# A linear-attention and MLP layer on one core: two token halves of a head scaled together and later, the first gate pass's block adds on VectorE, turned low parts issued later

## Chip, core and metric

The kernel runs on one core of a Trainium2 chip. TensorE multiplies matrices into PSUM, VectorE, ScalarE and GpSimd (POOL in the profile) work on SBUF and PSUM, and DMA queues move data; SP issues most DMAs. The metric is the device time in microseconds of one execution. Each engine runs its own instructions strictly in the order in which the program issued them; between engines they wait for each other's semaphores.

## What is computed

The reference, cut to what runs (DEPTH is 1, so the only layer is the gated linear attention, followed by the MLP and a last RMSNorm):

```python
def _gla_mixer(h, w_in, w_gate_up, b_gate, o_norm, w_out):
    proj = h @ w_in
    q, k, v, r, g_low = jnp.split(proj, [...], axis=-1)
    log_a = jax.nn.log_sigmoid((g_low @ w_gate_up + b_gate)) / GLA_GATE_TEMP
    ...
    def step(state, xs):                       # over chunks of 64 tokens
        q_c, k_c, v_c, d_c = xs
        state = d_c[..., None] * state + jnp.einsum('bhck,bhcv->bhkv', k_c, v_c)
        return state, jnp.einsum('bhck,bhkv->bhcv', q_c, state)
    ...
    o = o * lax.rsqrt(jnp.mean(o * o, axis=-1, keepdims=True) + EPS) * o_norm
    return (o * jax.nn.silu(r)) @ w_out

def reference(x, ...):
    h = x + _gla_mixer(_rmsnorm(x, gla_norm), ...)
    h = h + jnp.square(jax.nn.relu(_rmsnorm(h, mlp_norm) @ w_up)) @ w_down
    return _rmsnorm(h, final_norm)
```

256 tokens, model width 2048, 4 heads with 256 key and 512 value columns each, MLP width 8192, all in float32.

## The kernel before

**Products in three parts.** Every float32 weight is loaded raw and split in two: ScalarE casts it to a rounded *high* part, VectorE subtracts that from the raw weight for the *low* part. TensorE then multiplies high by high, low by high and high by low. A group of 512 weight rows x 512 columns (1 MB, the tile of 128 x 2048) is called a *double* in the code. A *plain* double is 48 matmuls of 256 columns. A *summed* double does the same with 42 after the scheme of Strassen and Winograd: it needs sums of the four 256-column blocks of the weights, and of the inputs.

**The stage of the change** begins where the projections q, k, v and the scores are done. It runs four passes over w_in for the gate r (c = 0 to 3, 512 columns each, 4 doubles per pass), then four over w_out. In this text the doubles are numbered in their order: 0 to 3 are pass 0 (0 and 2 plain, 1 and 3 summed), 4 to 7 pass 1 (plain), 8 to 11 pass 2 (8 and 10 plain, 9 and 11 summed), 12 to 15 pass 3 (plain), 16 and on w_out. The raw weights of double n go into `rawu0`, `rawu1` or `rawu2` (n mod 3; 2346, 2347 and 2348 in the order of instructions), its parts into `high` and `low` of three slots, also n mod 3. A load waits for the low part three doubles back, which is the last to read the raw tile.

**Summed doubles.** For each, POOL issues a DMA that adds one block to another within the raw tile (`add_block`, L843), then VectorE forms three sums (`adds`), ScalarE casts them into `sumshl`, and VectorE subtracts (`low`, L520). The high part of the whole raw tile also waits for the added block.

**Heads.** Between the steps of pass 0, TensorE computes the attention output of the four heads, each in two halves of 128 tokens (`attend`, 6 matmuls for half 0, 12 for half 1), every one into a PSUM bank of its own. For each half, `attend_square` lets ScalarE square it and sum the squares into `oss`; VectorE scales that one column; POOL raises it to -0.5 (`rsqrt`, L314, the *power*) and multiplies by `r1k` (L888, the *product*). `attend_put` then lets ScalarE write the scaled half into `on` (the *put*, L893) and gives the bank back. There are eight banks (named aux_1893, aux_1894, acc_1763 to acc_1766, acc_1895, acc_1896); they are handed out in the order in which they come back. Pass 0 holds four of them: t0, t1, b16 and b50.

**Combining.** At the end of a summed pass, `combine_parts` copies b16 (L932), adds and subtracts the banks on VectorE, and ScalarE applies silu (L965).

**Turned parts.** `on` and later h are transposed on TensorE; of each transposed block, ScalarE writes the high part and VectorE the low part (`put_turned`).

**What sets the order.** `at(time, run)` puts a piece of work into `plan`; the plan is sorted by time and issued in that order, and this is the order on every engine. The unit of time is one matmul. TensorE's steps stand in it from -LENGTH on; weights have fixed offsets to their use (high -75, low -56 for a plain double; high -67, low -50, sums -68 for a summed one).

Of the kernel before, what the change touches and what calls it, by code (L numbers as in the profile page):

```python
# [27 lines left out]
F32 = mybir.dt.float32  # L28
F32R = mybir.dt.float32r
AF = mybir.ActivationFunctionType  # L30
ALU = mybir.AluOpType

P = 128
T = 256
NT = T // P
# [4 lines left out]
DV = 512  # L40
# [30 lines left out]
def tile_gla_mlp(ctx, tc, x, xt, w_vg, w_in, w_gate, w_out, w_up, w_down, final_norm, out):  # L71
    nc = tc.nc
# [3 lines left out]
    st = ctx.enter_context(tc.tile_pool(name="st", bufs=4))  # L76
# [219 lines left out]
    r1k = const.tile([P, NT], F32, name="r1k")  # L296
# [16 lines left out]
    def rsqrt(dst, ms):  # L313
        nc.gpsimd.tensor_tensor(dst, ms, mhalf, op=ALU.pow)  # L314
# [303 lines left out]
    def at(time, run):  # L618
        plan.append((time, len(plan), run))
# [125 lines left out]
    def turned_part(key, n):  # L745
        return turn_banks[key][n // 2][:, n % 2 * T : (n % 2 + 1) * T]

    def put_turned(key, n, to, gain):
        s = turned_part(key, n)
        nc.scalar.activation(to[0], s, AF.Copy, scale=gain)  # L750
        nc.vector.scalar_tensor_tensor(to[1], s, gain, to[0].bitcast(F32), op0=ALU.mult, op1=ALU.subtract)
        if n % 2:
            banks.append(turn_banks[key][n // 2])
# [77 lines left out]
    for n, (p, c, g, summed_) in enumerate(doubles):  # L831
# [14 lines left out]
            chunk(key, time - UP_HI, time - UP_LO, time + 2 * UP, (time - UP_EARLY, load), raw)  # L846
            continue
        chunk(key, time - 67, time - 50, time + RAWS, (time - 165, load), raw)
        at(time - 116, add_block)

        def adds(view=view):
            add(sums[:, 0], view[:, :, 1, left], view[:, :, 0, left])
            add(sums[:, 1], sums[:, 0], view[:, :, 0, right])
            sub(sums[:, 2], sums[:, 0], view[:, :, 1, right])
# [23 lines left out]
        attend_state[hd, t] = o  # L878

    def attend_square(hd, t):  # L880
        o = attend_state[hd, t]
        ss = st.tile([P, 1], F32, tag="oss", name="oss")
        sq = tmp.tile([P, DV], F32, tag="t512", name="sq", bufs=3)
        nc.scalar.activation(sq, o, AF.Square, scale=r1k[:, t : t + 1], accum_out=ss)
        nc.vector.tensor_scalar(ss, ss, 1.0 / DV, EPS, op0=ALU.mult, op1=ALU.add)
        rs = st.tile([P, 1], F32, tag="ors", name="ors")
        rsqrt(rs, ss)
        nc.gpsimd.tensor_tensor(rs, rs, r1k[:, t : t + 1], op=ALU.mult)  # L888
        attend_state[hd, t] = o, rs

    def attend_put(hd, t):
        o, rs = attend_state[hd, t]
        nc.scalar.activation(on[:, t, hd * DV : (hd + 1) * DV], o, AF.Copy, scale=rs)  # L893
        banks.append(o)

    for hd, t, time in attend_at:
        at(time - LENGTH + 1, lambda hd=hd, t=t: attend_square(hd, t))
        at(time - LENGTH + 27, lambda hd=hd, t=t: attend_put(hd, t))


    def some512():
# [88 lines left out]
    def row_o(kt):  # L990
        return [a[:, OFF + kt * T : OFF + (kt + 1) * T] for a in (oth, otl)]
# [19 lines left out]

    e = mark("turn o0") + 16
    for n in range(8):
        at(e + 1 + 9 * n, lambda n=n: put_turned("o0", n, row_o(n), gain_o(n)))

    e = mark("turn o1") + 16
    for m, g in enumerate((2, 3)):
# [74 lines left out]
    def row_h(kt):  # L1092
        return [a[:, kt * T : (kt + 1) * T] for a in turned_h]
# [1 line left out]
    e = mark("turn h0") + 16  # L1095
    at(e - 17, take_h)
    for n in range(8):
        at(e + 1 + 9 * n, lambda n=n: put_turned("h0", n, row_h(n), g2(n)))

    def turn_h1():  # L1100
        bs = turn_banks["h1"] = [bank_in_parts() for _ in range(4)]
        for n, kt in enumerate(range(8, 16)):
            for t in range(NT):
                nc.tensor.transpose(bs[n // 2][:, n % 2 * T + t * P : n % 2 * T + (t + 1) * P], h[:, t, kt * P : (kt + 1) * P], ident)
        for n in (0, 2, 1, 3, 4, 6, 5, 7):
            put_turned("h1", n, row_h(8 + n), g2(8 + n))

    at(0.5, room_for_mlp)
    at(47.5, turn_h1)
# [478 lines left out]
```

## Time and profile before

| | |
|---|---|
| three runs | 1056.58, 1056.63, 1057.29 us; median 1056.63 |
| the profiled execution | 1056.8 us |
| its span, first to last instruction | 1055.0 us |
| mean granted TensorE clock | 0.997 |
| DMA, mean over the span | 217 GB/s |
| doubles 0 to 3 with the heads | TensorE from 190.81 us |

The profile names an instruction by line, engine, operation and tiles, output first; tile names are without their numbers there (`rawu` is any of the three). A wait is idle time of an engine, put down to what ended it. PEld is the loading of weights into TensorE, which runs beside the matmuls.

### The profile page before, as it was taken

How to read it: one execution, taken by the hardware profiler on the slowest of the kernel's cores; microseconds unless marked ns; L12 is line 12 of the kernel's file. 1: busy time of each engine (PE TensorE's matmuls, PEld its weight loads, DVE VectorE, ACT ScalarE, POOL GpSimd, SP SyncE). 2: the span in 40 equal slices, each digit the busy share in tenths (PEclk: the TensorE clock that was granted, in tenths of full speed). 3: DMA queues.
4: the chain of work that ended last, by engine and by line, in shares of the span. 5: the costliest groups of instructions: out<-in, count | busy, mean ns of one | idle time of the engine just before them, and what ended most of it. 6: DMA issues, size and time to landing. Idle time of an engine off the chain costs nothing.

```text
span 1055.0 us, 21250 instructions
## 1 busy us (share of the span) xinstructions
PE 1039.9 (99%) x9050; PEld 1037.9 (98%) x9050; DVE 848.1 (80%) x856; ACT 690.3 (65%) x824; POOL 101.7 (10%) x113
## 2 busy tenths in 40 slices
PE   9999999989999999999999999999999999999997
PEld 9999999989999999999999999999999999999997
DVE  6668657466767687799989989989999999899885
ACT  6675455474666565577776777767667767768753
POOL 0000000230000001001111011110101011010000
PEclk9999999999999999999999999999999999999999
DMA  9857664536767674788778787888788798787652
GB/s 341 307 164 219 189 192 159 141 120 185 263 216 216 178 267 139 238 247 233 227 225 257 217 241 227 224 249 238 213 241 231 219 262 228 201 258 228 202 189 99
DMA packets 118527, 229.27 MB, mean 217 GB/s; under 512 B 6256, under 2 KB 23664, under 8 KB 118304
## 3 DMA queue, kind: packets, MB, share of 16 engines
q1 hardware_dynamic: 99920, 208.84, 60.3%
q0 software_dynamic: 17408, 16.78, 10.3%
q10 hardware_dynamic: 1104, 2.29, 0.6%
q8 instruction: 70, 1.15, 0.4%
q14 instruction: 25, 0.20, 0.1%
HBM read 209.02 MB, written 2.10 MB: 200 GB/s over the span
## 4 chain that ended last, share of the span: by engine, by line
PE 85%; DVE 5%; DMA 4%; ACT 3%; issue 2%; POOL 1%; SPq 0%; POOLq 0%; ACTq 0%; DVEq 0%
PE acc L1223 29%; PE acc L1343 17%; PE acc L149 8%; PE acc L669 8%; PE aux L1343 7%; PE acc L181 6%; PE aux L1223 4%; DVE low L1187 2%; PE aux L181 2%; DMA raw<-in_w_vg 1%; DMA rawu<-rawu 1%; PE aux L669 1%; ACT high L1181 1%; POOL ors L314 1%; DMA rawu<-in_w_down 1%
## 5 line engine op out<-in xcount | busy, mean ns | idle before, releaser
L1223 PE MATMUL acc<-hh,high 128*128 128x256 f32 x896 | 247.6, 276 | 0.0
L1223 PE MATMUL acc<-hh,low 128*128 128x256 f32 x896 | 247.5, 276 | 0.0
L1223 PE MATMUL acc<-hl,high 128*128 128x256 f32 x896 | 247.5, 276 | 0.0
L1187 DVE TENSOR_TENSOR low<-rawu,high 128x2048 fp32r<-128x2048 f32 (+1 forms) x101 | 224.5, 2225 | 22.5 <-ACT high L1181 20.6
L1181 ACT CAST high<-rawu 128x2048 fp32r<-128x2048 f32 (+1 forms) x101 | 187.2, 1857 | 49.4 <-DMA rawu<-rawu 21.5
L1223 PEld LDWEIGHTS acc<-hh,high 128*128 128x128 f32 x896 | 168.3, 188 | 0.0
L1223 PEld LDWEIGHTS acc<-hh,low 128*128 128x128 f32 x896 | 168.3, 188 | 0.0
L1223 PEld LDWEIGHTS acc<-hl,high 128*128 128x128 f32 x896 | 168.3, 188 | 0.0
L1392 ACT CAST sumshl<-sums 128x1024 fp32r<-128x1024 f32 x112 | 88.3, 834 | 93.0 <-PE acc L1343 61.1
L1187 DVE TENSOR_TENSOR low<-rawd,high 128x2048 fp32r<-128x2048 f32 (+1 forms) x59 | 132.7, 2251 | 17.7 <-ACT high L1181 17.7
L1181 ACT CAST high<-rawd 128x2048 fp32r<-128x2048 f32 (+1 forms) x59 | 111.5, 1891 | 46.3 <-PE acc L1223 29.2
L520 DVE TENSOR_TENSOR sumshl<-sums,sumshl 128x1536 fp32r<-128x1536 f32 x64 | 112.3, 1754 | 26.5 <-ACT sumshl L1392 25.4
L1379 POOL DMA_DIRECT2D rawd<-rawd x56 | 67.6, 1207 | 514.5 <-DVE sums L519 218.2
L119 DVE TENSOR_TENSOR lo<-raw,hi 128x1024 fp32r<-128x1024 f32 (+3 forms) x68 | 78.6, 1163 | 42.5 <-ACT hi L118 42.1
L118 ACT CAST hi<-raw 128x1024 fp32r<-128x1024 f32 (+3 forms) x68 | 67.6, 1001 | 53.8 <-PE acc L181 25.7
L1343 PE MATMUL acc<-high,acts 128*128 128x256 f32 x510 | 101.7, 276 | 0.0
L1343 PEld LDWEIGHTS acc<-high,acts 128*128 128x128 f32 x510 | 83.6, 188 | 0.0
L1343 PE MATMUL acc<-sumshl,acts 128*128 128x256 f32 x600 | 80.7, 276 | 0.0
L1343 PEld LDWEIGHTS acc<-sumshl,acts 128*128 128x128 f32 x600 | 73.8, 188 | 0.0
L1343 PE MATMUL acc<-low,acts 128*128 128x256 f32 x255 | 70.4, 276 | 0.0
L181 PE MATMUL acc<-xl,hi 128*128 128x256 f32 x192 | 53.0, 276 | 0.0
L181 PE MATMUL acc<-xh,lo 128*128 128x256 f32 x192 | 53.0, 276 | 0.0
(351 smaller groups left out, 2587.9 us busy)
## 6 DMA issues: line engine op xcount, KB each, us to landing
rawu<-in_w_up SPq DMA_DIRECT2D x124, 512.0 KB, 4.6
rawd<-in_w_down SPq DMA_DIRECT2D x56, 1024.0 KB, 5.2
raw<-in_w_in SPq DMA_DIRECT2D x48, 512.0 KB, 4.6
rawu<-in_w_in SPq DMA_DIRECT2D x16, 1024.0 KB, 5.2
rawu<-in_w_out SPq DMA_DIRECT2D x16, 1024.0 KB, 5.4
rawd<-rawd POOLq DMA_DIRECT2D x56, 256.0 KB, 5.2
rawu<-in_w_down SPq DMA_DIRECT2D x16, 512.0 KB, 4.6
raw<-in_w_vg SPq DMA_DIRECT2D x13, 520.0 KB, 8.3
```

What stands on the lines that cost most here:

```text
L118: last_hi[0] = nc.scalar.copy(hi[:, s], raw[:, s])
L119: last_lo[0] = nc.vector.tensor_tensor(lo[:, s], raw[:, s], hi[:, s].bitcast(F32), op=ALU.subtract)
L149: nc.tensor.matmul(o[:, m], x, w[:, m], start=first and c == 0, stop=last, skip_group_check=True)
L181: nc.tensor.matmul(o, u[:, s], m[:, kt], start=kt == 0 and n == 0 and j % 2 == 0, stop=kt == KT - 1 and n == 2, skip_group_check=True,)
L520: sub = lambda o, x, y: nc.vector.tensor_tensor(o, x, y, op=ALU.subtract)
L669: nc.tensor.matmul(b[:, o], a[x], w[y], start=(pc, name) in fresh, stop=last and i == 2, skip_group_check=True)
L1181: nc.scalar.copy(o, i)
L1187: nc.vector.tensor_tensor(o, i, x.bitcast(F32), op=ALU.subtract)
L1223: nc.tensor.matmul(o, w[:, s], row_h(kt)[m], start=kt == 0 and n == 0 and j % 2 == 0, stop=kt == KT - 1 and n == 2, skip_group_check=True,)
L1343: nc.tensor.matmul(bank[:, o], a[x], w[y], start=fresh and i == 0, stop=d + 1 in starts + [SUMMED] and i == 2, skip_group_check=True,)
L1379: nc.gpsimd.dma_start(out=view[:, :, 1, left], in_=view[:, :, 1, right], accum_op=ALU.add)
L1392: nc.scalar.copy(sums_to[0][:, f], sums[:, f])
```

## The change

Three edits:
- Each head's two halves get one tile of two columns for the sums of squares. The square of each half stays where it was; once, 14 units behind half 1, VectorE scales both columns, POOL does two powers and one product of two columns. The puts come 46 and 50 units behind half 1; before, each came 27 behind its own half.
- For pass 0 of the gate (doubles 1 and 3), the added block is formed by VectorE ahead of the three sums; the POOL DMA stays for all other summed doubles.
- The turned low parts of o0 and h0 are put into the plan 6 units behind their high parts, and not together with them.

```diff
@@ -745,9 +745,11 @@
     def turned_part(key, n):
         return turn_banks[key][n // 2][:, n % 2 * T : (n % 2 + 1) * T]
 
-    def put_turned(key, n, to, gain):
+    def put_turned_high(key, n, to, gain):
+        nc.scalar.activation(to[0], turned_part(key, n), AF.Copy, scale=gain)
+
+    def put_turned_low(key, n, to, gain):
         s = turned_part(key, n)
-        nc.scalar.activation(to[0], s, AF.Copy, scale=gain)
         nc.vector.scalar_tensor_tensor(to[1], s, gain, to[0].bitcast(F32), op0=ALU.mult, op1=ALU.subtract)
         if n % 2:
             banks.append(turn_banks[key][n // 2])
@@ -846,9 +848,13 @@
             chunk(key, time - UP_HI, time - UP_LO, time + 2 * UP, (time - UP_EARLY, load), raw)
             continue
         chunk(key, time - 67, time - 50, time + RAWS, (time - 165, load), raw)
-        at(time - 116, add_block)
-
-        def adds(view=view):
+        here = (p, c) == ("r", 0)
+        if not here:
+            at(time - 116, add_block)
+
+        def adds(view=view, here=here):
+            if here:
+                add(view[:, :, 1, left], view[:, :, 1, left], view[:, :, 1, right])
             add(sums[:, 0], view[:, :, 1, left], view[:, :, 0, left])
             add(sums[:, 1], sums[:, 0], view[:, :, 0, right])
             sub(sums[:, 2], sums[:, 0], view[:, :, 1, right])
@@ -878,24 +884,33 @@
         attend_state[hd, t] = o
 
     def attend_square(hd, t):
-        o = attend_state[hd, t]
-        ss = st.tile([P, 1], F32, tag="oss", name="oss")
+        if t == 0:
+            attend_state[hd] = st.tile([P, NT], F32, tag="oss", name="oss", bufs=2)
         sq = tmp.tile([P, DV], F32, tag="t512", name="sq", bufs=3)
-        nc.scalar.activation(sq, o, AF.Square, scale=r1k[:, t : t + 1], accum_out=ss)
+        nc.scalar.activation(
+            sq, attend_state[hd, t], AF.Square, scale=r1k[:, t : t + 1], accum_out=attend_state[hd][:, t : t + 1]
+        )
+
+    def attend_scale(hd):
+        ss = attend_state[hd]
         nc.vector.tensor_scalar(ss, ss, 1.0 / DV, EPS, op0=ALU.mult, op1=ALU.add)
-        rs = st.tile([P, 1], F32, tag="ors", name="ors")
-        rsqrt(rs, ss)
-        nc.gpsimd.tensor_tensor(rs, rs, r1k[:, t : t + 1], op=ALU.mult)
-        attend_state[hd, t] = o, rs
+        rs = attend_state[hd, "rs"] = st.tile([P, NT], F32, tag="ors", name="ors", bufs=2)
+        for t in range(NT):
+            rsqrt(rs[:, t : t + 1], ss[:, t : t + 1])
+        nc.gpsimd.tensor_tensor(rs, rs, r1k, op=ALU.mult)
 
     def attend_put(hd, t):
-        o, rs = attend_state[hd, t]
-        nc.scalar.activation(on[:, t, hd * DV : (hd + 1) * DV], o, AF.Copy, scale=rs)
+        o, rs = attend_state[hd, t], attend_state[hd, "rs"]
+        nc.scalar.activation(on[:, t, hd * DV : (hd + 1) * DV], o, AF.Copy, scale=rs[:, t : t + 1])
         banks.append(o)
 
     for hd, t, time in attend_at:
-        at(time - LENGTH + 1, lambda hd=hd, t=t: attend_square(hd, t))
-        at(time - LENGTH + 27, lambda hd=hd, t=t: attend_put(hd, t))
+        a = time - LENGTH
+        at(a + 1, lambda hd=hd, t=t: attend_square(hd, t))
+        if t:
+            at(a + 14, lambda hd=hd: attend_scale(hd))
+            for i in range(NT):
+                at(a + 46 + 4 * i, lambda hd=hd, i=i: attend_put(hd, i))
 
 
     def some512():
@@ -1011,7 +1026,8 @@
 
     e = mark("turn o0") + 16
     for n in range(8):
-        at(e + 1 + 9 * n, lambda n=n: put_turned("o0", n, row_o(n), gain_o(n)))
+        for wait, put in ((1, put_turned_high), (7, put_turned_low)):
+            at(e + wait + 9 * n, lambda n=n, put=put: put("o0", n, row_o(n), gain_o(n)))
 
     e = mark("turn o1") + 16
     for m, g in enumerate((2, 3)):
@@ -1095,7 +1111,8 @@
     e = mark("turn h0") + 16
     at(e - 17, take_h)
     for n in range(8):
-        at(e + 1 + 9 * n, lambda n=n: put_turned("h0", n, row_h(n), g2(n)))
+        for wait, put in ((1, put_turned_high), (7, put_turned_low)):
+            at(e + wait + 9 * n, lambda n=n, put=put: put("h0", n, row_h(n), g2(n)))
 
     def turn_h1():
         bs = turn_banks["h1"] = [bank_in_parts() for _ in range(4)]
@@ -1103,7 +1120,8 @@
             for t in range(NT):
                 nc.tensor.transpose(bs[n // 2][:, n % 2 * T + t * P : n % 2 * T + (t + 1) * P], h[:, t, kt * P : (kt + 1) * P], ident)
         for n in (0, 2, 1, 3, 4, 6, 5, 7):
-            put_turned("h1", n, row_h(8 + n), g2(8 + n))
+            for put in (put_turned_high, put_turned_low):
+                put("h1", n, row_h(8 + n), g2(8 + n))
 
     at(0.5, room_for_mlp)
     at(47.5, turn_h1)
```

What this does to the order on the engines. POOL, from the start of pass 0 on, before: two DMAs, and a power and a product for each of the eight halves (`oss` and `ors` have a number of their own each).

```order
L843 DMA rawu1_2347<-rawu1_2347 128x2x256
L314 TENSOR_TENSOR ors_2426<-oss_2422,mhalf_116 128x1
L888 TENSOR_TENSOR ors_2426<-ors_2426,r1k_127 128x1
L314 TENSOR_TENSOR ors_2484<-oss_2480,mhalf_116 128x1
L888 TENSOR_TENSOR ors_2484<-ors_2484,r1k_127 128x1
L843 DMA rawu0_2346<-rawu0_2346 128x2x256
L314 TENSOR_TENSOR ors_2518<-oss_2514,mhalf_116 128x1
L888 TENSOR_TENSOR ors_2518<-ors_2518,r1k_127 128x1
```

The same place on POOL in the changed kernel, down to the first DMA, which is that of double 9.

```order
L314 TENSOR_TENSOR ors_2479<-oss_2422,mhalf_116 128x1 x2
L900 TENSOR_TENSOR ors_2479<-ors_2479,r1k_127 128x2
L314 TENSOR_TENSOR ors_2557<-oss_2507,mhalf_116 128x1 x2
L900 TENSOR_TENSOR ors_2557<-ors_2557,r1k_127 128x2
L314 TENSOR_TENSOR ors_2642<-oss_2582,mhalf_116 128x1 x2
L900 TENSOR_TENSOR ors_2642<-ors_2642,r1k_127 128x2
L314 TENSOR_TENSOR ors_2730<-oss_2671,mhalf_116 128x1 x2
L900 TENSOR_TENSOR ors_2730<-ors_2730,r1k_127 128x2
L845 DMA rawu0_2346<-rawu0_2346 128x2x256
```

Both DMAs ahead of double 9's are gone, and the four heads follow one another. VectorE from double 1's low part on, before:

```order
L1187 TENSOR_TENSOR low1_2350<-rawu1_2347,high1_2349 128x2048
L885 TENSOR_SCALAR oss_2422<-oss_2422 128x1
L520 TENSOR_TENSOR sumshl_2357<-sums_2345,sumshl_2357 128x1536
L885 TENSOR_SCALAR oss_2480<-oss_2480 128x1
L1187 TENSOR_TENSOR low2_2352<-rawu2_2348,high2_2351 128x2048
L885 TENSOR_SCALAR oss_2514<-oss_2514 128x1
L519 TENSOR_TENSOR sums_2345<-rawu0_2346 128x512
```

The same stretch of VectorE in the changed kernel:

```order
L1205 TENSOR_TENSOR low1_2350<-rawu1_2347,high1_2349 128x2048
L520 TENSOR_TENSOR sumshl_2357<-sums_2345,sumshl_2357 128x1536
L1205 TENSOR_TENSOR low2_2352<-rawu2_2348,high2_2351 128x2048
L896 TENSOR_SCALAR oss_2422<-oss_2422 128x2
L519 TENSOR_TENSOR rawu0_2346<-rawu0_2346 128x2x256
L519 TENSOR_TENSOR sums_2345<-rawu0_2346 128x512
```

The scale of head 0 has gone behind double 2's low part, and the new add stands ahead of double 3's sums. ScalarE from head 2's first square on (aux_1893 and aux_1894 are head 2's banks, acc_1765 and acc_1766 those of heads 1 and 3, acc_1763 is b16 of pass 0), before:

```order
L884 ACTIVATE sq_2593,oss_2592<-aux_1893,r1k_127 128x512
L1181 CAST high1_2349<-rawu1_2347 128x2048
L893 ACTIVATE on_1999<-aux_1893,ors_2596 128x512
L884 ACTIVATE sq_2652,oss_2651<-aux_1894,r1k_127 128x512
L893 ACTIVATE on_1999<-aux_1894,ors_2655 128x512
L884 ACTIVATE sq_2686,oss_2685<-acc_1765,r1k_127 128x512
L1181 CAST high2_2351<-rawu2_2348 128x2048
L932 COPY sums_2345<-acc_1763 128x512
```

The same stretch of ScalarE in the changed kernel; high1 is double 4's high part, high2 double 5's.

```order
L890 ACTIVATE sq_2583,oss_2582<-aux_1893,r1k_127 128x512
L904 ACTIVATE on_1999<-acc_1765,ors_2557 128x512
L904 ACTIVATE on_1999<-acc_1766,ors_2557 128x512
L1199 CAST high1_2349<-rawu1_2347 128x2048
L890 ACTIVATE sq_2638,oss_2582<-aux_1894,r1k_127 128x512
L890 ACTIVATE sq_2672,oss_2671<-acc_1765,r1k_127 128x512
L1199 CAST high2_2351<-rawu2_2348 128x2048
L904 ACTIVATE on_1999<-aux_1893,ors_2642 128x512
L947 COPY sums_2345<-acc_1763 128x512
L904 ACTIVATE on_1999<-aux_1894,ors_2642 128x512
```

The puts of head 1 now stand ahead of double 4's high part, and those of head 2 behind double 5's; the square of head 3's first half stands ahead of them. Since banks come back in another order, TensorE's double 4 has the banks aux_1893 and acc_1763, where it had aux_1893 and aux_1894. TensorE's matmuls and SP's loads keep their order throughout. On VectorE and ScalarE, nothing changes its place for o0; for h0, one turned low part goes behind a weights' low part.

## The prediction

> **What bounds the kernel now.** I read the page's busy line first, then the busy time of the engines by stretches, then TensorE's own timeline in the stretches that are not full, and last the chain of waits there. The columns of a stretch are its length and each engine's busy time and instructions, then the granted clock.
>
> ```profile
> PE 1039.9 (99%) x9050; PEld 1037.9 (98%) x9050; DVE 848.1 (80%) x856; ACT 690.3 (65%) x824; POOL 101.7 (10%) x113
> ...
> 152.00:192.00 40.00, 40.00 (x348) 40.00 (x347) 26.48 (x41) 20.55 (x31) 1.36 (x1) 1.00 0.54 165
> 192.00:250.00 58.00, 53.23 (x436) 52.62 (x436) 31.14 (x34) 31.43 (x42) 17.15 (x18) 0.97 0.49 154
> 250.00:300.00 50.00, 48.22 (x409) 47.81 (x408) 36.45 (x37) 30.18 (x32) 1.22 (x1) 1.00 0.65 217
> 300.00:392.00 92.00, 92.00 (x812) 92.00 (x811) 71.62 (x68) 55.72 (x68) 4.83 (x4) 1.00 0.68 209
> 392.00:1000.00 608.00, 608.00 (x5362) 608.00 (x5360) 540.32 (x461) 432.66 (x481) 70.64 (x59) 1.00 0.79 229
> ```
>
> TensorE is full from 300 to 1000 us. Whatever is won before 300 is therefore carried to the end, and an edit behind 300 that nobody waits for is worth nothing. All of the change but the turned parts of h lies between 184 and 290 us, where TensorE has holes. These are its rows there: start, length, instruction, and in brackets the idle time before it and who ended it.
>
> ```profile
> 205.36 0.28 PE L669 MATMUL acc<-high,xh 128*128 128x256 f32 x1
> 208.18 0.28 PE L149 MATMUL aux<-vh,at 128*128 128x256 f32 x1
> 213.13 0.28 PE L669 MATMUL acc<-high,xh 128*128 128x256 f32 x1
> 215.82 0.38 PE L669 MATMUL acc<-low,xh 128*128 128x256 f32 x1 [2.41 <-DVE low L1187]
> 217.71 0.41 PE L669 MATMUL acc<-low,xh 128*128 128x256 f32 x1
> 224.39 0.28 PE L669 MATMUL aux<-high,xh 128*128 128x256 f32 x1
> 225.77 0.38 PE L669 MATMUL aux<-high,xh 128*128 128x256 f32 x1 [0.52 <-ACT on L893]
> 238.60 0.38 PE L669 MATMUL aux<-low,xh 128*128 128x256 f32 x1 [1.84 <-DVE low L1187]
> 256.31 0.39 PE L669 MATMUL acc<-low,xh 128*128 128x256 f32 x1 [0.48 <-DVE low L1187]
> 286.46 0.38 PE L669 MATMUL acc<-low,xh 128*128 128x256 f32 x1 [1.30 <-DVE low L1187]
> ```
>
> Between 205.36 and 208.18 stand 24 matmuls: 0.1175 us each. A hole costs its idle time and 0.16 us more, since a matmul of 0.28 us is normally followed after 0.12. Double 3 begins at 213.13 and double 4 at 224.39; between them are 60 matmuls, 7.05 us at that pace, so 4.21 us are lost: 2.57 of waiting, the rest because matmuls after the hole ran at half speed (0.41 us at 217.71). The other holes cost 0.67 (225.77 instead of 224.39 + 6 x 0.1175), 2.00, 0.64 and 1.46 us. **All holes together: 9.0 us.** More than this cannot be won here.
>
> **The first hole and what feeds it.** Double 3 waits for its low part, and that for the add of the blocks, which is a DMA issued by POOL:
>
> ```profile
> 200.50 2.28 DVE L1187 TENSOR_TENSOR low<-rawu,high 128x2048 fp32r<-128x2048 f32 x1
> 200.67 2.52 POOL L314 TENSOR_TENSOR ors<-oss,mhalf 128x1 f32<-128x1 f32 x1 [1.66 <-DVE oss L885]
> 203.50 0.69 ACT L893 ACTIVATE on<-aux,ors 128x512 f32<-128x512 f32 x1 [3.09 <-POOL ors L888]
> 204.08 0.68 ACT L884 ACTIVATE sq<-acc,r1k 128x512 f32<-128x512 f32 x1
> 204.65 0.20 ACT L884 ACTIVATION_READ_ACCUMULATOR sq<-acc,r1k 128x1 f32 x1
> 210.78 1.92 ACT L1181 CAST high<-rawu 128x2048 fp32r<-128x2048 f32 x1 [4.10 <-DMA rawu<-rawu]
> ...
> 203.79 6.93 DMA rawu<-rawu
> ```
>
> The DMA starts at 203.79 because POOL was busy with a power until 203.19, and lands at 210.72. The high part follows on ScalarE, then the low part on VectorE. With the add on VectorE the DMAs of doubles 1 and 3 go, and their 6.9 us with them. In their place stand two adds of 128 x 512 elements. The sums of the same size show the price:
>
> ```profile
> 190.92 1.91 ACT L1181 CAST high<-rawu 128x2048 fp32r<-128x2048 f32 x1
> 191.72 0.68 DVE L519 TENSOR_TENSOR sums<-rawu 128x512 f32<-128x512 f32 x1
> 194.31 2.28 DVE L1187 TENSOR_TENSOR low<-rawu,high 128x2048 fp32r<-128x2048 f32 x1
> 210.80 0.69 DVE L519 TENSOR_TENSOR sums<-rawu 128x512 f32<-128x512 f32 x1 [5.76 <-DMA rawu<-rawu]
> ```
>
> Double 1 pays: its add runs at 191.72 to 192.41, its high part starts at 192.44 instead of 190.92, and its low part (after the last value part, which moves too) ends at 197.9 instead of 196.6. TensorE reaches double 1 at 205.36 - 60 x 0.1175 = 198.3, so 0.4 us of double 0's matmuls still cover it: cost 0, or up to 0.7 if my hand-offs are short.
>
> **The heads.** Per head there is now one scale on VectorE for two columns, two powers and one product on POOL, and the two puts on ScalarE come later. What a power costs depends on its neighbour (the first row is a product):
>
> ```profile
> 203.27 0.19 POOL L888 TENSOR_TENSOR ors<-ors,r1k 128x1 f32<-128x1 f32 x1
> 226.73 0.55 POOL L314 TENSOR_TENSOR ors<-oss,mhalf 128x1 f32<-128x1 f32 x1 [1.73 <-DVE oss L885]
> ...
> 401.14 1.23 DVE L1187 TENSOR_TENSOR low<-rawd,high 128x1024 fp32r<-128x1024 f32 x1 [0.58 <-ACT high L1181]
> ...
> 401.14 2.36 DVE L1187 TENSOR_TENSOR low<-rawd,high 128x1024 fp32r<-128x1024 f32 x2 [0.58 <-ACT high L1181]
> ...
> 401.19 1.58 POOL L314 TENSOR_TENSOR r<-ms,mhalf 128x1 f32<-128x1 f32 x1
> ```
>
> Alone it takes 0.55 us. Beside a low part it ends 0.41 us behind that: the power of 200.67 at 203.19, behind the low part that ends at 202.78; the one of 401.19 at 402.77, behind 402.37. A second low part stood right behind the one of 401.14 (two in 2.36 us), and POOL still came through between them. So I let each power, and the product, wait for the VectorE operation that already runs, not for those behind it. The Trainium skill ("SBUF — State Buffer", "Who interferes with whom") has this as a rule: a VectorE operation with two SBUF inputs and a GpSimd operation that reads SBUF exclude each other for a whole instruction, and the earlier one wins. The rows agree.
>
> On before's clock this gives, with 1.8 us from one high part to the next instruction, 2.28 for a low part, 0.69 for a put, 0.68 + 0.20 for a square and its sum:
> - Head 0: the scale stands behind double 2's low part, which no scale holds up any more and which ends at 201.8 instead of 202.8. Behind it come double 3's four adds, to 204.6, and POOL's three steps slip between them: 202.9, 203.6, 204.05. Puts until 205.3, double 3's high part 205.2 to 207.1, its low part until 210.2 instead of 215.8. TensorE needs it at 213.1. **The first hole and the slow clock go: 4.2 us.**
> - Head 1: square at 207.0, scale at 207.85, powers behind low 3 (210.6) and behind the sums' low part (212.25), product 212.5, puts until 213.8, high 4 until 215.6, low 4 at 217.9, needed at 220.2.
> - Head 2: scale at 217.85, powers 218.6 and 219.2, product from 219.3 to 219.5. High 5 must wait for the square of head 3's first half, whose matmuls end at 213.13 + 29 x 0.1175 + 0.28 = 216.8; it ends at 219.4, and low 5 starts at 219.5. The product is 0.2 us ahead of it.
> - Double 4 wants its first bank at 213.13 + 7.05 = 220.2. That is head 2's first bank, put at 219.5 to 220.2. Its second bank is now the b16 of pass 0, copied out (L932) by 220.7 and wanted at 220.9. In place of the 0.67 us hole a bank wait of about **0.3 us** stays (bounds 0 and 3.0, the upper one below).
>
> **Behind that**, double 6, 9 and 14, with the rows that set them:
>
> ```profile
> 230.42 0.42 DVE L520 TENSOR_TENSOR sums<-sums 128x256 f32<-128x256 f32 x1
> 232.91 0.69 DVE L519 TENSOR_TENSOR sr<-acc,sums 128x512 f32<-128x512 f32 x1
> ...
> 234.33 1.90 ACT high L1181
> 236.25 2.30 DVE low L1187
> 238.57 5.03 DMA rawu<-in_w_in
> 244.16 7.70 DMA rawu<-rawu
> ...
> 253.96 2.29 DVE low L1187
> ...
> 284.12 2.30 DVE low L1187
> ```
>
> - Double 6: low 5 ends at 221.8, the combining of pass 0 takes 3.2 us (230.42 to 233.60), the second silu 0.7 (as long as a put), the high part 1.9, the low part 2.3: 229.9. TensorE arrives at 220.5 + 96 x 0.1175 = 231.8. The 2.00 us hole goes.
> - Double 9: its load waits for that low part. From there to the landing of its own POOL add it took 238.57 to 251.86, 13.3 us; now 229.9 + 13.3 = 243.2. Its low part ended 4.4 us after the landing: 247.6. TensorE arrives at 220.5 + 240 x 0.1175 = 248.7. The 0.64 us go.
> - Double 14: from that landing VectorE and ScalarE work without a pause until 286.42, 34.6 us. Now 243.2 + 34.6 = 277.8. TensorE needs it 28.7 us behind double 9 (256.31 to 286.46, less 1.46), at 277.5. Of 1.46 us, 0.2 to 0.3 stay.
>
> The turned low parts cost and bring nothing: for o0 no instruction changes its place on any engine, and for h0 one turned low part goes behind a weights' low part, at a time when TensorE is full. VectorE's load hardly changes: 1.4 us more for two adds, and four of eight small scales less.
>
> **Sum:** 9.0 - 0.3 - 0.2 = 8.5 us. The profiled execution took 1056.8 us (span 1055.0), the runs' median is 1056.63. 1056.8 - 8.5 = **1048.3 us**.
>
> **The rivals.**
> - *The product of head 2 is caught.* If POOL is 0.2 us later, low 5 starts first and holds the product until 221.8, or, if the second power is caught too, until 222.5. The put then ends at 222.6 to 223.2 and TensorE waits 2.4 to 3.0 us for the bank. A hole of 2.57 us brought the half clock here, one of 2.00 did not (238.60 is followed by the usual pace), so 0 to 1.6 us come on top. Double 14 then waits no more. Gain 9.0 - (2.4 to 4.6) = 4.4 to 6.6: 1050.2 to 1052.4 us. The Trainium skill ("TensorE: Matmul & The Clock Gate", "What's actually happening") lets the clock fall only after an idle window of some 3.4 us; by that the case would end at 1050.2 to 1050.8. The half clock after 2.57 us speaks against it. For this rival: 0.2 us is little after a dozen hand-offs. Against: ScalarE's wait for TensorE, which sets low 5, is sure.
> - *POOL does not come between, and every power takes 2.5 us.* Five of the eight powers took 1.9 to 2.5 us before, each beside a long operation. A head then costs 2 x 2.52 + 0.26 = 5.3 us. Head 0 ends at 207.1, low 3 at 213.2; head 1 at 216.3, and head 3's first bank is 1.0 us late; low 4 is 0.4 late; head 2 ends at 227.0, its bank comes 6.1 us late; with 1.6 of slow clock the loss is 9.1, no gain: 1056.8. This is the point from which the change is slower: each 0.5 us more per power adds 3 us, 1059.8 at 3.0. Against it: the row of 401.19.
> - *Given back at double 9.* Its DMA is now POOL's first in this stage. If it lands as late as before, at 251.9, TensorE waits 7.6 us at double 9, and with the slow clock all is lost again: 1056.8; half of the delay would leave 1052 to 1053. Nothing in the profile asks for it, as the landing follows the load.
> - *That the change doesn't do what it says* holds for the turned parts, and is in every case.
>
> **How the numbers follow.** The first case has 0.55, the caught product 0.27, the slow powers 0.08, the giving back 0.10. The forecast is the first, 1048.3. Its bounds: 9.0 us of holes plus 0.8 for pace give 1047.0; the caught product's end, with some of the giving back, 1052.8. What is left out has less than 0.2. A measurement here can tell 0.2%, 2.1 us. Faster: 0.55 + 0.27 + 0.05 (half of the giving back) = 0.87. Same: 0.05 of the slow powers and 0.04 = 0.09. Slower: 0.04.
>
> **What would show it.** Right: no DMA by POOL before double 9; double 3's first matmul without idle time and no matmul of 0.41 us behind it; double 4 about 4.2 us earlier, its hole named "on" and under 0.5 us; double 6 and 9 without a hole; double 14 some 8.5 us earlier. The caught product would show as a product of about 2.5 us on POOL and a hole of over 2 us at double 4. Wrong: a new hole at double 1 (197.9 against 198.3), or double 9's landing less than 6 us earlier.

## Result, and the profile after

The changed kernel takes **1063.8 us** (median of 6 runs, 1063.13 to 1064.3); the kernel before, beside it, 1056.61 (6 runs, 1055.59 to 1057.29). The ratio is 1.0068, with a 95% interval of 1.0055 to 1.0081: slower by 0.7%, where 0.8% faster had been forecast and slower had a chance of 0.04.

The stage of the change came out as forecast all the same. These are the only hole that is left in TensorE's timeline between 192 and 300 us, and POOL's work there from head 2 on:

```profile
278.21 0.39 PE L669 MATMUL acc<-low,xh 128*128 128x256 f32 x1 [1.69 <-DVE low L1205]
```

```profile
218.59 1.06 POOL L314 TENSOR_TENSOR ors<-oss,mhalf 128x1 f32<-128x1 f32 x2 [5.58 <-DVE oss L896]
219.73 0.20 POOL L900 TENSOR_TENSOR ors<-ors,r1k 128x2 f32<-128x2 f32 x1
226.34 1.14 POOL L314 TENSOR_TENSOR ors<-oss,mhalf 128x1 f32<-128x1 f32 x2 [6.42 <-ACT sr L980]
227.56 0.20 POOL L900 TENSOR_TENSOR ors<-ors,r1k 128x2 f32<-128x2 f32 x1
236.31 1.35 POOL L845 DMA_DIRECT2D rawu<-rawu  x1 [8.55 <-DVE low L1205]
```

Double 14 starts at 278.21 and not at 286.46: 8.25 us are won. POOL's first DMA is that of double 9. The loss lies behind, where the sum put nothing. Below are the stretches of after (length, busy time of PE, PEld, DVE, ACT and POOL with their instructions, granted clock, DMA share, GB/s), and two of before, cut at the same places:

```profile
PE 1051.1 (99%) x9050; PEld 1050.7 (99%) x9050; DVE 849.9 (80%) x854; ACT 690.0 (65%) x824; POOL 93.4 (9%) x107
...
140.00:190.00 50.00, 50.00 (x422) 50.00 (x421) 30.17 (x47) 23.18 (x37) 0.00 (x0) 1.00 0.53 169
192.00:250.00 58.00, 58.00 (x505) 58.00 (x504) 38.84 (x40) 38.68 (x49) 11.41 (x14) 1.00 0.53 156
250.00:300.00 50.00, 48.31 (x421) 48.11 (x421) 36.96 (x39) 29.19 (x36) 0.00 (x0) 1.00 0.72 250
300.00:392.00 92.00, 92.00 (x795) 92.00 (x795) 69.61 (x69) 56.63 (x74) 4.83 (x4) 1.00 0.66 207
400.00:1000.00 600.00, 600.00 (x5191) 600.00 (x5191) 527.39 (x442) 416.75 (x456) 67.59 (x56) 1.00 0.78 227
```

```profile
140.00:190.00 50.00, 50.00 (x435) 50.00 (x435) 31.11 (x49) 24.35 (x39) 1.36 (x1) 1.00 0.57 174
400.00:1000.00 600.00, 600.00 (x5292) 600.00 (x5291) 534.57 (x453) 425.15 (x466) 70.64 (x59) 1.00 0.79 229
```

Read the counts beside PE. TensorE is busy for all of the 600 us in both, at a granted clock of 1.00, but it does 5191 matmuls where it did 5292. It is not idle, it is slower. 101 matmuls at 0.1134 us (600 / 5292) are 11.5 us.

By product, only one half of the MLP is slow, the last product (activations by w_down). In the timelines of before and of after, the last product's row of 18 equal matmuls reads:

```profile
639.83 2.20 PE L1343 MATMUL acc<-sumshl,acts 128*128 128x256 f32 x18
```

```profile
636.89 2.29 PE L1361 MATMUL acc<-sumshl,acts 128*128 128x256 f32 x18
```

With 0.28 us for the last matmul, 17 steps take 1.92 us in the one and 2.01 in the other: 0.113 and 0.118 us per matmul. Taken from the starts of all matmuls of such runs, the two paces are 0.1133 and 0.1178. They come back in everything below.

**What differs is where the tiles lie.** The two small tiles of a head got `bufs=2`, and had four before. In the built programs each such buffer takes 32 bytes of a partition, whether it holds one column or two, so their pool shrank by 128 bytes, and every tile that is allocated behind it on the same side moved:

```
first byte in the partition   before   after
xh, hh (turned x, turned h)    27392   27264
at, extra, rawd                68864   68736
acts                           97536   97408
oth                           118528  118400
high0 (weights, other side)   135424  135424
```

A matmul has a *loaded* input of 128 columns (the weights of PEld) and a *moving* one of 256. Their starts are called here by their place in 256 bytes (a tile's use begins up to 192 bytes behind its first byte). In before, nearly all loaded inputs start at byte 192 and the moving ones at 0: a distance of 192. In after, xh, oth and acts start at 64, while the weights stay.

### The profile page after: what moved, and what is told of

The parts are those of the page before. It is cut to its first block, busy times and chain, and to the rows that moved or that the text cites. A ratio compares the mean times of both kernels' runs of the same rounds, so it can differ in the third digit from the quotient of the medians.

```text
span 1061.3 us, 21237 instructions
## 1 busy us (share of the span) xinstructions
PE 1051.1 (99%) x9050; PEld 1050.7 (99%) x9050; DVE 849.9 (80%) x854; ACT 690.0 (65%) x824; POOL 93.4 (9%) x107
## 4 chain that ended last, share of the span: by engine, by line
PE 93%; DVE 3%; ACT 1%; DMA 1%; issue 1%; POOLq 0%; POOL 0%; ACTq 0%; DVEq 0%
PE acc L1361 22%; PE acc L1241 17%; PE aux L1241 16%; PE acc L149 11%; PE acc L669 9%; PE acc L181 6%; PE aux L1361 4%; PE aux L669 2%; PE aux L181 2%; PE aux L149 2%; DVE low L1205 2%; ACT high L1199 1%; DMA rawu<-rawu 1%; DMA rawu<-in_w_in 0%; PE aux L216 0%
## 5 line engine op out<-in xcount | busy, mean ns | idle before, releaser
L1241 PE MATMUL acc<-hh,high 128*128 128x256 f32 x544 | 150.5, 277 | 0.0
L1241 PE MATMUL acc<-hh,low 128*128 128x256 f32 x544 | 150.4, 277 | 0.0
L1241 PE MATMUL acc<-hl,high 128*128 128x256 f32 x544 | 150.4, 277 | 0.0
L1241 PE MATMUL aux<-hh,high 128*128 128x256 f32 x480 | 133.2, 278 | 0.0
L1241 PE MATMUL aux<-hl,high 128*128 128x256 f32 x480 | 133.0, 277 | 0.0
L1241 PE MATMUL aux<-hh,low 128*128 128x256 f32 x480 | 133.0, 277 | 0.0
L1241 PEld LDWEIGHTS acc<-hh,high 128*128 128x128 f32 x544 | 102.2, 188 | 0.0
L1241 PEld LDWEIGHTS acc<-hh,low 128*128 128x128 f32 x544 | 102.2, 188 | 0.0
L1241 PEld LDWEIGHTS acc<-hl,high 128*128 128x128 f32 x544 | 102.2, 188 | 0.0
L1361 PE MATMUL acc<-sumshl,acts 128*128 128x256 f32 x720 | 99.4, 281 | 0.0
```

The source lines that it names most:

```text
L1241: nc.tensor.matmul(o, w[:, s], row_h(kt)[m], start=kt == 0 and n == 0 and j % 2 == 0, stop=kt == KT - 1 and n == 2, skip_group_check=True,)
L1361: nc.tensor.matmul(bank[:, o], a[x], w[y], start=fresh and i == 0, stop=d + 1 in starts + [SUMMED] and i == 2, skip_group_check=True,)
```

## The experiments

**The pool restored.** In the changed kernel, both tiles keep the pool's four buffers:

```diff
-            attend_state[hd] = st.tile([P, NT], F32, tag="oss", name="oss", bufs=2)
+            attend_state[hd] = st.tile([P, NT], F32, tag="oss", name="oss")
-        rs = attend_state[hd, "rs"] = st.tile([P, NT], F32, tag="ors", name="ors", bufs=2)
+        rs = attend_state[hd, "rs"] = st.tile([P, NT], F32, tag="ors", name="ors")
```

> The changed kernel, but with four buffers instead of two for the sums of squares (oss) and for their factors (ors), so that their pool is as large as in the kernel before and every later tile lies at the address it had there; nothing else differs. Theory (the addresses): with two buffers the pool shrank by 128 bytes per partition, and the inputs that are loaded into TensorE as weights (xh, oth, hh, acts) went from byte 192 to byte 64 of a 256-byte line; TensorE's own pace fell with it from 0.1133 to 0.1178 us per matmul in the last MLP product. With the addresses restored the pace from 400 to 1000 us is 0.1133 again and the time 1056.6 - 8.3 = 1048.3 us. Rival (the change's order of work, or the won time itself, slows TensorE): 1063.8 us and a pace of 0.1178, as in the changed kernel.

Measured: 1047.44 us (1047.03 to 1047.67), ratio 0.9921 (0.9909 to 0.9934) to the kernel before. Its stretches:

```profile
140.00:190.00 50.00, 50.00 (x436) 50.00 (x435) 31.11 (x50) 24.84 (x40) 0.00 (x0) 1.00 0.52 169
192.00:250.00 58.00, 58.00 (x496) 57.97 (x495) 38.74 (x39) 39.49 (x49) 11.40 (x14) 1.00 0.54 163
...
300.00:392.00 92.00, 92.00 (x812) 92.00 (x812) 70.63 (x72) 58.62 (x78) 5.40 (x6) 1.00 0.66 207
400.00:1000.00 600.00, 600.00 (x5293) 600.00 (x5292) 536.76 (x451) 427.33 (x467) 67.60 (x56) 1.00 0.80 232
```

The some 16 us to the changed kernel hang on the number of buffers alone. At 0.1133 us each, the 102 matmuls more from 400 to 1000 us are 11.6 of them, 17 from 300 to 392 are 1.9 and 14 from 140 to 190 are 1.6; from 192 to 250 the changed kernel does 9 more, 1.0 us the other way. The rest lies between these stretches and behind 1000 us.

**The same 128 bytes taken from the kernel before**, by two buffers instead of four for two tiles that are used twice at its very end; no instruction moves:

```diff
-            some = st.tile([P, 1], F32, tag="some", name="some")
+            some = st.tile([P, 1], F32, tag="some", name="some", bufs=2)
-            rf = st.tile([P, 1], F32, tag="rf", name="rf")
+            rf = st.tile([P, 1], F32, tag="rf", name="rf", bufs=2)
```

> The kernel before, but with two buffers instead of four for two small tiles that are used twice at its very end (some, rf): no instruction moves, and the same tiles as in the changed kernel lie 128 bytes lower. Theory (the addresses): the matmuls lose what the changed kernel lost, 7.2 us of net loss plus 8.3 us won in the stage of the change = 15.5 us: 1072 us, with 0.1178 us per matmul in the last MLP product. Rival (the order of work, or the won time, slows TensorE): 1056.6 us.

Measured: 1072.37 us, ratio 1.0156 (1.0142 to 1.017). Its row in the last product is that of after:

```profile
645.26 2.29 PE L1343 MATMUL acc<-sumshl,acts 128*128 128x256 f32 x18
```

Without any change of order the kernel loses 1.6%, some 16 us. The rivals, by which the order of work or the won time slows TensorE, are out.

**Half of the shift** (`bufs=2` for the factors alone):

> The changed kernel with four buffers for the sums of squares and two for the factors: the pool shrinks by 64 bytes only, and the inputs loaded into TensorE lie at byte 128 of a 256-byte line. Theory (the addresses): the few tiles that lie at byte 0 or 128 in both kernels run at 0.118 to 0.123 us per matmul, so the loss is as large as in the changed kernel or larger, 1064 to 1080 us. If the loss grew evenly with the shift it would be about half, 1056 us. Rival (not the addresses): 1063.8 us, with 0.1178 in the last MLP product.

Measured: 1092.74 us, ratio 1.035 (1.0336 to 1.0364), above all that was expected. From 400 to 1000 us:

```profile
400.00:1000.00 600.00, 600.00 (x5032) 600.00 (x5032) 515.89 (x433) 402.65 (x442) 68.21 (x57) 1.00 0.76 218
```

The first MLP product is slow here too, at 0.120 us (from the starts of its matmuls): there the weights are loaded, from byte 192, and the turned h moves, now also from byte 192, a distance of 0.

**Which tile of the MLP?** The activations moved back (e4), the raw weights and the activations (e5), all inputs of TensorE (e6), all of the MLP's tiles (e7). The edits of e6, of which e4 has the second and third, with the same 32 floats for the two blocks of activations that lie behind the turned h:

```diff
-        turned_h.extend(turnp.tile([P, KT * ROW + 64], F32R, tag="A" + i, name="h" + i) for i in "hl")
+        turned_h.extend(turnp.tile([P, KT * ROW + 64], F32R, tag="A" + i, name="h" + i)[:, 32:] for i in "hl")
-        most = room_in(mlp, 10 * n + 64, "acts", F32R)
+        most = room_in(mlp, 10 * n + 80, "acts", F32R)
-        places += [most[:, OFF + i * n : OFF + (i + 1) * n] for i in range(10)]
+        places += [most[:, OFF + 32 + i * n : OFF + 32 + (i + 1) * n] for i in range(10)]
```

and the one of e5 (e7 has it with the first line of e6):

```diff
+        room_in(mlp, 32, "gap")
```

> The changed kernel with only the MLP's activations (acts, the inputs of the last product) put 128 bytes further within their tiles, back to byte 192 of a 256-byte line; all other tiles stay 128 bytes lower than in the kernel before. Theory (the addresses, and only those of the inputs loaded into TensorE): the last product's 2352 matmuls run at 0.1133 instead of 0.1178 us again, 10.8 us less: 1053.0 us; the earlier stages stay slow. Rival (not the addresses): 1063.8 us.

> The changed kernel with 32 unused floats ahead of the MLP's own tiles: the raw weights of the last product (rawd), the sums that are kept and the activations (acts) lie again where they lay in the kernel before; the turned h (hh, hl) stays 128 bytes lower. The activations alone moved back brought nothing (1062.5). If what counts there is the address of the raw weights, which DMA writes and ScalarE and VectorE read beside TensorE, the last product runs at 0.1133 again and the time is 1063.8 - 10.8 = 1053.0 us. If what counts is the turned h, by which TensorE comes into the last product in another rhythm, or what happened before the MLP, it stays at 1062 to 1064 us.

> The changed kernel with the turned h (hh, hl) and the activations (acts) put 128 bytes further within their tiles: every input of TensorE in the MLP lies where it lay in the kernel before, while the raw weights (rawd) and the kept sums stay 128 bytes lower. If TensorE's own inputs set the pace and carry it from one product into the next, 1053.0 us with 0.1133 in the last product; if it is the raw weights beside it, or what happened before the MLP, 1062 to 1064 us.

> The changed kernel with both edits: everything that the MLP touches lies where it lay in the kernel before; only what stands ahead of the MLP stays 128 bytes lower. If addresses count where they are used, the MLP is as fast as before: 1053.0 us, with the value pass (140 to 190 us) still at 0.1178. If the slow pace is carried on from the stages ahead of the MLP, 1062 to 1064 us.

Measured: e4 1062.52, e5 1063.22, e6 **1051.16**, e7 **1050.08** us. The first expectation missed: with the activations back at byte 192 next to nothing came back. With the turned h moved as well, the last product's pace came back whole. The last product's row in e4, and then in e6:

```profile
627.30 2.28 PE L1361 MATMUL acc<-sumshl,acts 128*128 128x256 f32 x18
```

```profile
624.10 2.20 PE L1361 MATMUL acc<-sumshl,acts 128*128 128x256 f32 x18
```

These 18 matmuls have the same two inputs at the same addresses in both kernels. What differs among TensorE's inputs is the product that runs ahead of them, whose moving input is the turned h. So moving back the raw weights, which DMA, ScalarE and VectorE touch, brings nothing that can be told (e5), and a matmul's own addresses don't settle its pace.

**Matmuls alone.** The layer left out; 48 matmuls for each of 32 pairs of starts, in order, shuffled, and beside loads, casts and subtractions:

> No part of the layer is computed: 96 stretches of 48 matmuls of the kernel's kind (128x128 against 128x256), in the order high, low, high of a plain double, with the start of the loaded input at each multiple of 32 bytes in 256 and that of the moving input at 0, 64, 128 and 192; 32 stretches in order, the same 32 shuffled, and the same 32 beside loads, casts and subtractions of weights. If the addresses of TensorE's own inputs set its pace, the stretches differ by some 4% (0.1133 to 0.1178 us per matmul), by address and alike in the three passes. If the pace hangs on what the other engines do, only the third pass is slow. If it is carried over from what ran before, the first two passes differ for the same addresses.

Measured in one run, by the distance from the start of the moving input to that of the loaded one (12 stretches each, from the starts of their matmuls at the full clock):

```
bytes, in 256    us per matmul
0                0.120
32               0.118
64               0.113 to 0.114 (7 stretches), 0.118 (5)
96               0.117 to 0.120
128              0.119 to 0.120
160              0.120
192              0.118
224              0.117 to 0.118
```

In the main the distance counts, in whatever way it is made up. At 64 there are two paces for the same addresses. Loaded 192 and moving 128 ran at 0.1178 in the first pass and at 0.1133 in the shuffled one, which is one matmul more in 5 us:

```profile
144.50:149.50 5.00, 5.00 (x45) 5.00 (x44) 0.00 (x0) 0.00 (x0) 0.00 (x0) 1.00 0.00 0
281.00:286.00 5.00, 5.00 (x46) 5.00 (x45) 0.00 (x0) 0.00 (x0) 0.00 (x0) 1.00 0.00 0
508.00:513.00 5.00, 5.00 (x45) 5.00 (x44) 3.03 (x2) 1.91 (x1) 0.00 (x0) 1.00 0.78 283
```

The third row is the pass beside the other engines. It agrees with the first pass in 30 of the 32 pairs, so their work isn't what sets the pace in the main. The two other pairs (loaded 64 and 96, moving 0) went from 0.1133 to 0.1178 and from 0.120 to 0.1174; why stays open. Distance 192, which was fast in the kernel, was never fast here.

**The pace that is carried over.** Stretches at 192 and at 64, each behind 24 matmuls at another distance; then holes:

> No part of the layer is computed: stretches of 48 matmuls whose loaded input lies 192 bytes behind the moving one (as in the kernel before) or 64 (as in the changed kernel), each behind 24 matmuls at another distance (0 to 224 bytes, by 32), twice; then four holes of some us in a stretch at 192. If the pace is carried on by what ran before, the same 48 matmuls run at 0.1133 behind some distances and at 0.1178 behind others, alike in both repeats: by the run with the pool restored, at 0.1133 behind 0 and at 0.1178 behind 128. If a matmul's own addresses set its pace, all 48 are alike whatever ran ahead. If a hole turns the fast pace into the slow one, as it seemed at 219 us of the run with h moved, the matmuls behind the holes run at 0.1178.

Measured, again in one run: at 192, 0.1133 behind 64 in both repeats; 0.1178 behind 96, 128, 160 and 224 in both. Behind 32 it was 0.1178 in the first repeat and 0.1133 in the second, which is the pace that TensorE had ahead of the 32; behind 0 it was 0.1178 at the kernel's start, with the clock still at half, and then 0.1133. All stretches at 64 ran at 0.113 to 0.114. Here are stretches at 192 behind 64, behind 128, behind 32 in the second repeat, and behind 32 in the first:

```profile
40.00:45.00 5.00, 5.00 (x47) 5.00 (x46) 0.00 (x0) 0.00 (x0) 0.00 (x0) 1.00 0.02 3
57.00:62.00 5.00, 5.00 (x45) 5.00 (x44) 0.00 (x0) 0.00 (x0) 0.00 (x0) 1.00 0.01 3
166.00:170.00 4.00, 4.00 (x38) 4.00 (x37) 0.00 (x0) 0.00 (x0) 0.00 (x0) 1.00 0.00 0
32.50:36.50 4.00, 4.00 (x36) 4.00 (x35) 0.00 (x0) 0.00 (x0) 0.00 (x0) 1.00 0.00 0
```

Three of the four holes were followed by more matmuls at 192 (0.30, 2.27 and 3.97 us of idle time). All three turned 0.1133 into 0.1178; this is the matmul behind the shortest:

```profile
296.03 0.39 PE L94 MATMUL acc<-movh,stath 128*128 128x256 f32 x1 [0.30 <-ACT acc L105]
```

The fourth, of 1.62 us, is followed in the built program by 21 matmuls at distance 0; they took 0.120 us each, and 192 behind them ran at 0.1133.

**The parts of the change, each alone, with the layout of before.** p1 is the second edit of the change on the kernel before; p2 the first one, without `bufs=2`:

> The kernel before with one part of the change: pass 0's added blocks formed by VectorE; every tile lies where it lay. By the prediction's own sum the first hole goes, 4.2 us, since low 3 ends near 209.5 and is needed at 213.1, and with it a part of the holes that hang on it: 1050 to 1052 us. If the heads' small steps on POOL make the hole, it stays in part: 1054 to 1056.5 us.

> The kernel before with one part of the change: each head's halves scaled together and later, but with four buffers for the two small tiles, so that every tile lies where it lay; pass 0's blocks are still added by POOL's DMA. If the heads make the holes, most of the win is here: 1049 to 1051 us. If the DMA makes the first one, it stays and little is won: 1053 to 1056.5 us.

Measured: p1 1053.84 us (1051.62 to 1055.06, ratio 0.9978, 0.9969 to 0.9987), which is ahead of its second case and behind its first; p2 **1047.72** (ratio 0.9923, 0.991 to 0.9936). The heads alone bring what both bring (1047.44); beside them the adds on VectorE bring nothing that can be told. POOL in p2 shows why:

```profile
183.63 1.35 POOL L843 DMA_DIRECT2D rawu<-rawu  x1 [61.28 <-DVE low L1196]
189.82 1.21 POOL L843 DMA_DIRECT2D rawu<-rawu  x1 [4.84 <-DMA rawu<-in_w_in]
...
200.26 1.57 POOL L314 TENSOR_TENSOR ors<-oss,mhalf 128x1 f32<-128x1 f32 x2 [9.24 <-DVE oss L890]
```

With the powers later, the DMA of double 3 isn't queued behind them: it goes at 189.82 and not at 203.79.

The adds alone take the first hole as well, but for 0.22 us, and the half clock with it, but not the holes behind it. In p1's profiled execution these are rows with idle time at doubles 3, 4 and 14; a hole of 1.94 us at double 6 (235.41) stays too:

```profile
216.66 0.86 PE L669 MATMUL acc<-sumshl,h 128*128 128x256 f32 x5 [0.22 <-DVE sumshl L520]
...
221.18 0.39 PE L669 MATMUL aux<-low,xh 128*128 128x256 f32 x1 [0.72 <-DVE low L1191]
...
282.64 0.38 PE L669 MATMUL acc<-low,xh 128*128 128x256 f32 x1 [1.29 <-DVE low L1191]
```

**Faster still?** With the pool restored, TensorE is slow from the first summed input of the gate on (in the buffer of h, distance 128) until the copies in `extra` (distance 0). c1 moves the former to 192, c2 the latter too:

```diff
-    x_forms = {g: sums_of_rows(hbuf[:, OFF + n * 2 * G : OFF + (n + 1) * 2 * G]) for n, g in enumerate((2, 3))}
+    x_forms = {g: sums_of_rows(hbuf[:, OFF + 16 + n * 2 * G : OFF + 16 + (n + 1) * 2 * G]) for n, g in enumerate((2, 3))}
```

```diff
-        return extra[:, :G].rearrange("p (n i t) -> p n i t", n=2, i=2)
+        return extra[:, OFF : G + OFF].rearrange("p (n i t) -> p n i t", n=2, i=2)
```

> The changed kernel with its pool restored (1047.4 us), and the summed inputs of the gate, which lie in the buffer of h at byte 128 of a 256-byte line in all kernels so far, moved by 64 bytes to byte 192, as all the others. In the run with the pool restored, TensorE ran at 0.1133 us per matmul until the first matmul with these inputs at 198.3, and at 0.1178 from there to 256.9 and from 260.4 to 298.7, also in matmuls whose own inputs lie at byte 192. If the pace is carried on by what ran before, these 97 us are run at 0.1133 and 97 x 0.039 = 3.8 us go: 1043.6 us. If each matmul's pace hangs on its own addresses alone, only the 90 or so matmuls with these inputs gain 0.005 us each: 1047.0 us.

> The same, and the copies of eight blocks of the gate's and the output's inputs (extra) moved from byte 0 to byte 192: their 72 matmuls ran at 0.120 us. If the slow pace comes in only by inputs at another byte, none is left and 72 x 0.0067 = 0.5 us more go: 1043.1 us. If these matmuls at byte 0 are needed to bring the pace back to 0.1133 (it came back right behind them at 256.9 and 298.7), for instance after the transposes, the pace stays at 0.1178 for longer and the time is above that of the run before this one.

Measured: c1 1049.05 us (1046.95 to 1050.46), above both of its cases, though two of its six runs took 1047.0 and 1047.1, its second case; c2 1052.75 us, its second case. Two things are to be seen. First c1, then c2, from 304 to 340 us, where both run matmuls with the same addresses:

```profile
304.00:340.00 36.00, 36.00 (x320) 36.00 (x319) 30.10 (x28) 21.26 (x21) 1.91 (x2) 1.00 0.74 220
```

```profile
304.00:340.00 36.00, 36.00 (x308) 36.00 (x307) 29.01 (x29) 22.05 (x23) 2.34 (x2) 1.00 0.71 207
```

In c2 the matmuls of the copies are no longer at distance 0, and the fast pace doesn't come back until the MLP. The other is c1's timeline at head 2 (c2 has the same hole of 2.43 us, at 221.52):

```profile
218.80 2.29 DVE L1205 TENSOR_TENSOR low<-rawu,high 128x2048 fp32r<-128x2048 f32 x1 [0.83 <-ACT high L1199]
...
219.19 1.95 POOL L900 TENSOR_TENSOR ors<-ors,r1k 128x2 f32<-128x2 f32 x1
...
221.92 0.52 PE L669 MATMUL aux<-high,xh 128*128 128x256 f32 x1 [2.43 <-ACT on L904]
```

This is the prediction's rival of the caught product, at its place and its price (2.4 us of hole, and matmuls at half clock behind it). d1 therefore raises both columns in one operation:

```diff
-        for t in range(NT):
-            rsqrt(rs[:, t : t + 1], ss[:, t : t + 1])
+        nc.gpsimd.tensor_tensor(rs, ss, mhalf.to_broadcast([P, NT]), op=ALU.pow)
```

> The run with h moved (1049.1 us), with both powers of a head in one POOL operation of two columns. There TensorE kept 0.1133 us up to 219 us, then waited 2.4 us for a bank, since head 2's product came 0.4 us behind the start of a low part on VectorE and was held until its end; half the clock and the pace of 0.1178 followed until 258. With one power of 0.55 us in place of two in 1.06 the product starts at 218.7, ahead of the low part at 218.8: no hole, 2.4 + 1.6 us less, and 35 us at the faster pace, 1.4 us: 1043.7 us. If the product is caught all the same, or the power of two columns takes as long as two: 1049 us.

Measured: **1047.0 us** (1046.12 to 1047.81; ratio 0.9919, 0.9905 to 0.9933), between its two cases. The long hole is gone, but not the slow pace, which now begins behind a stall of 0.1 us (the matmul of 218.56, 0.38 long and 0.2 behind the one ahead of it). A part of what TensorE gains, it waits for at double 14, and behind another stall near the end the slow pace comes in again:

```profile
218.56 0.38 PE L669 MATMUL aux<-high,xh 128*128 128x256 f32 x1
...
276.27 0.39 PE L669 MATMUL acc<-low,xh 128*128 128x256 f32 x1 [1.14 <-DVE low L1204]
...
1018.48 0.50 PE L149 MATMUL aux<-high,acts 128*128 128x256 f32 x2 [0.38 <-DVE h L519]
```

With the pool restored alone, the wait at double 14 is 0.43 us, and double 14 starts at 277.24. So d1 is 0.97 us ahead there; in its profiled execution this lead is gone behind the stall of 1018.48, where TensorE does 155 matmuls in 18 us (1020 to 1038) and ahead of it 160 (1000 to 1018). So d1 and the changed kernel with its pool restored are alike, and both beat both kernels.

## Why the prediction was wrong

- **The step that failed** is its first: "TensorE is full from 300 to 1000 us. Whatever is won before 300 is therefore carried to the end, and an edit behind 300 that nobody waits for is worth nothing." It takes a full engine for one at a fixed pace. The win was carried to 300 and then given back, 8.25 us and 7.2 more. What the runs showed in its place: TensorE stays full from 400 to 1000 us and yet does 5191 matmuls for 5292, at 0.1178 us and not 0.1133 in the last product; with the tiles where they lay, it does 5293 (e1). The signs stood in its own rows: 812 matmuls in 92.00 us are 0.1133 each, and the 24 that it counted at 0.1175 ran at the same granted clock. Two paces at one clock were used without being asked about, and the range had 0.8 us for pace as a gain alone.
- **The term that is missing** from the sum is `bufs=2`. The change was worked through as instructions that move; that it also moves tiles was not priced, though the kernel pads its tiles (OFF = 48). None of the rivals had it.
- **The mechanism in the stage held.** Sum 8.5, measured 8.25 at double 14. Double 3, 4, 6 and 9 have no hole; the product of head 2 came through (219.73, low 5 at 220.13). At double 14, 1.69 us stay and not 0.2 to 0.3: TensorE arrives sooner, being at 0.1133 in parts of this stage. With the addresses held, the ratio of 0.9921 puts the median at 1048.3, the forecast; the interval leaves 1.3 us either way, so agreement to the last digit is luck.
- **Which edit wins** was half right. The first hole was credited to the DMA that goes. Without that DMA it does go (p1), but the heads alone remove it too, since they clear POOL's queue ahead of the DMA (p2), and only they remove the holes at doubles 4 and 6. The turned low parts were not tried alone.
- **The rival of the caught product** was rightly placed and priced: in the changed kernel the product was 0.40 us ahead of low 5 (219.73 and 220.13), in c1 0.39 us behind it, and caught.

**What stays open** is what the carried pace is. In the changed kernel the value pass (140 to 190 us) and the last product are slow at distance 64, at which m2 was always fast and m1 slow in 5 of 12 stretches, and in e4 a distance of 192 is slow behind 64. The moving start changes there as well, which m2 doesn't vary. From a distance alone the pace can't be told.

## What to carry over

Divide busy time by instructions in every stage, before and after: a busy engine can lose time without a single wait. Before a scheduling edit is priced, ask whether it changes the size of a pool, and compare the tiles' addresses; to measure such an edit, hold them. Where one layout runs fast, put small tiles where their number of buffers can't move TensorE's inputs.

## Of the hardware, unexpected

- Matmuls of 128x128 by 128x256 take 0.1133 to 0.120 us at one granted clock, by the distance of their inputs' starts in 256 bytes, and at 64 and 192 either 0.1133 or 0.1178 with the same addresses; at 192 it followed what ran before (m2).
- Behind a stall of 0.1 to 0.4 us the fast pace can turn into the slow one: for the 48 matmuls that followed in m2 (296.03, 0.30 us of idle time), for some 30 us in d1 (218.56).
- A hole of 2.43 us brought the half clock (c1, 221.92), as one of 2.41 did in the kernel before; one of 2.27 in m2 did not, one of 3.97 there did.
